# Layer-norm sums as rows, VectorE in place of GpSimd, and turns and moves in fours

## The chip, the cores and the metric

One Trainium2 chip, one of its cores. The kernel is one program with one launch; the metric is its device time in microseconds (us). The core has five engines with instruction streams of their own: TensorE (PE) for matrix products, VectorE (DVE), ScalarE (ACT), GpSimd (POOL) and SyncE (SP), which here issues the loads of weights. A profiled execution has a trace of all of them.

## What is computed

One decoder layer on 256 tokens with 16 meta tokens ahead of them (T = 272), width 2048, all in float32. Cut to what matters here:

```
h = concat(meta, x)
q, c_kv, q_idx, k_idx, w_idx, u = split_columns(h @ w_in)
c_kv = rms_norm(c_kv, kv_norm_g)                # per token, over 256 channels
...                                             # sparse attention, multi-scale pooling
mix = concat(attn_out, pool_out) @ w_o
h = layer_norm(ALPHA * h + mix, ln1_g, ln1_b)   # per token, over 2048 channels
z = causal depthwise conv of width 3 over tokens (h @ w_up) + conv_b
f = (gelu(z[:, :FF]) * z[:, FF:]) @ w_down      # FF = 5632
out = layer_norm(ALPHA * h + f, ln2_g, ln2_b)[16:]
```

`rms_norm` divides by the root of the mean square, `layer_norm` subtracts the mean and divides by the standard deviation; both need, for each token, sums over all channels.

## The kernel before

**Layout.** Activations lie transposed: channels on the 128 partitions, tokens along the free dimension. `y[:, m, :]` is the m-th of 16 tiles of 128 channels. From the output projection on, NQ = 258 token columns are kept (two of the meta tokens, for the convolution, and the 256). A sum over channels is therefore a sum over partitions.

**Products.** Each float32 operand is split into a rounded upper part and a remainder, and a product is three matmuls (upper by upper, upper by lower, lower by upper): `product`, L195 to L197, 16 channel tiles deep, so 48 matmuls per block. Weights stream from HBM in tiles of 1 MB in a fixed order (`stream`); SP loads a tile, ACT makes the upper halves (L123) and DVE the lower ones (L124), two pieces of each per tile. `weights()` hands out the next tile and starts the work on the one two ahead; there are three buffers for raw tiles and three for split ones. `behind(i)` is a context: what is issued inside it on ACT or DVE is put behind the split of tile i on that engine. For the rest the instructions' order on each engine is laid out when the program is built, by priority and modelled readiness, and is not exactly that of the code. Each engine then works through its order.

**The RMS norm of the latent.** `latent_scale` (after the first indexer block) squares two channel tiles and sums them over partitions with `column_sums`: the tile is the stationary operand, a block of 64 ones moves, so that the sums of up to 128 tokens come out with tokens on partitions; three cuts of tokens make a 128x3 tile. `pow(-0.5)` on POOL gives the scale. `latent_norm` (one block later) turns this into a row of all tokens on every partition with `spread`: products of the broadcast scale with the identity.

**The first layer norm** is folded into the first four pairs of up-projection blocks (FOLDED = 4; a pair is f, with half 0 and 1 of the gate). `about_k(m)` subtracts a rough mean, adds the tile to `s1` and its square to `s2` (two halves of one buffer `sums`, on POOL), and makes the operand `folded`, scaled by the norm's gain. PE can then start the first up blocks before mean and deviation are known. In the first of them, after 8 of the 16 channel tiles, `deviation()` sums `s1` and `s2` over partitions (`column_sums`, L242), and computes mean and 1/deviation with tokens on partitions; after 15 tiles `deviation_rows()` spreads both with L248 and ACT copies them (L696) to `rs` and `m2`, halves of `of_token`. Two things follow from them. `normalise(m)` makes the true h of tile m: POOL multiplies by `rs` (L704), DVE adds `m2` (L705), ACT applies gain and bias (L706) and splits (L708), DVE subtracts (L709); three tiles per block, behind the next split. `unfold(ps)` corrects a folded block: DVE multiplies by `rs` (L732), ACT makes `w` from `m2` (L734), POOL adds (L735). From f = 4 on, blocks use the true h.

**Turns and moves.** The residual for the second norm has tokens on partitions. DVE turns each 32x32 block of y (L886, after the gates of f = 4 and 5, eight tiles each), and 32 DMAs on ACT's queue (`residual`, L716) move the blocks to `y2`; six, five and five of them after the gates of f = 6 to 11. Then the down projection adds to `y2` with a fast scheme of seven products (`seven`, L787 to L789, L795).

Of the kernel before, what the change touches and what calls it, by code (L numbers as in the profile page):

```python
# [11 lines left out]
F32 = mybir.dt.float32  # L12
F32R = mybir.dt.float32r
AF = mybir.ActivationFunctionType
# [3 lines left out]
P = 128  # L18
# [24 lines left out]
REPLACED = -3e38  # L43
KA = NM + P
KB = T
KW = KA + KB
STRIP = 400
G_KV, G_POOL, LN1, C_W, C_B, N_COLS = 0, 2, 10, 42, 306, 394
# [19 lines left out]
def tile_layer(ctx, tc, xt, w_first, w_proj, w_uk, w_uv, w_pool, w_o, w_up, w_down, cols, rows, rel_bias, onehot, out):  # L68
# [163 lines left out]
    half = sb.tile([P, 3], F32, name="half")  # L232
    nc.vector.memset(half, -0.5)

    def col(base, j):
        return cv[:, base + j:base + j + 1]

    def column_sums(s, cuts, j, ps):

        for i, (a, b) in enumerate(cuts):  # L240
            for n, t in enumerate(s):
                nc.tensor.matmul(ps[:b - a, 64 * (3 * j + i):64 * (3 * j + i) + 64], t[:, a:b], ones[:, :64],  # L242
                                 start=n == 0, stop=n == len(s) - 1)

    def spread(r, cuts, rb):

        for i, (a, b) in enumerate(cuts):
            nc.tensor.matmul(rb[:, a:b], r[:b - a, i:i + 1].to_broadcast([b - a, P]), ident[:b - a, :b - a],  # L248
                             start=True, stop=True)

    def temp(shape, name):
        return ap_.tile(shape, F32, tag="t", name=name, bufs=4, padded_shape=[P, KW])
# [35 lines left out]
    for j in range(2):  # L288
        ps = heads[1 + j][0]
        nc.scalar.activation(ct[:, j, :], ps[:, :T], AF.Copy)  # L290
        sq = temp([P, T], "sq")
        nc.scalar.activation(sq, ps[:, :T], AF.Square)
        sqs.append(sq)
    widx = ap_.tile([P, 2, HI], F32, name="widx")
    ps = small()
# [5 lines left out]
    cuts = ((0, P), (P, 2 * P), (2 * P, T))  # L301
    v = sb.tile([P, 3], F32, name="rms_v")

    def latent_scale():
        ps = small()
        column_sums(sqs, cuts, 0, ps)
        nc.vector.memset(v, 1.0)
        for i, (a, b) in enumerate(cuts):
            nc.vector.tensor_scalar(v[:b - a, i:i + 1], ps[:b - a, 64 * i:64 * i + 1], 1.0 / C, EPS,
                                    op0=ALU.mult, op1=ALU.add)  # L310
# [322 lines left out]
    of_token = fp.tile([P, 2 * NQ], F32, name="of_token", tag="u2", bufs=1)  # L633
    rs, m2 = of_token[:, :NQ], of_token[:, NQ:]
    folded = []

    def about_k(m):
# [32 lines left out]
                about_k(len(folded))  # L670


    cuts = ((0, P), (P, 2 * P), (2 * P, NQ))
    st = fp.tile([P, 4, 3], F32, name="st", bufs=1)
    nc.vector.memset(st, 1.0)

    def deviation():
        ps = small()
        column_sums([s1], cuts, 0, ps)
        column_sums([s2], cuts, 1, ps)  # L680
        for i, (a, b) in enumerate(cuts):
            r = slice(0, b - a)
            nc.vector.tensor_scalar_mul(st[r, 0, i:i + 1], ps[r, 64 * i:64 * i + 1], 1.0 / D)
            nc.vector.tensor_scalar(st[r, 1, i:i + 1], ps[r, 64 * (3 + i):64 * (3 + i) + 1], 1.0 / D, EPS,
                                    op0=ALU.mult, op1=ALU.add)
        nc.vector.tensor_tensor(st[:, 2, :], st[:, 0, :], st[:, 0, :], op=ALU.mult)
        nc.vector.tensor_tensor(st[:, 1, :2], st[:, 1, :2], st[:, 2, :2], op=ALU.subtract)
        nc.vector.tensor_tensor(st[:2, 1, 2:], st[:2, 1, 2:], st[:2, 2, 2:], op=ALU.subtract)
        nc.gpsimd.tensor_tensor(st[:, 2, :], st[:, 1, :], half, op=ALU.pow)
        nc.vector.scalar_tensor_tensor(st[:, 3, :], st[:, 0, :], -1.0, st[:, 2, :], op0=ALU.mult, op1=ALU.mult)  # L690

    def deviation_rows():
        for j, dst in ((2, rs), (3, m2)):
            ps = small()
            spread(st[:, j, :], cuts, ps)
            nc.scalar.activation(dst, ps[:, :NQ], AF.Copy)  # L696


    y2 = fp.tile([P, 2, D], F32, name="y2", bufs=1)
# [1 line left out]

    def normalise(m):
        yd = y[:, m, Q0:]
        nc.gpsimd.tensor_tensor(yd, yd, rs, op=ALU.mult)  # L704
        nc.vector.tensor_tensor(yd, yd, m2, op=ALU.add)  # L705
# [3 lines left out]
        nc.vector.tensor_tensor(a[:, 1, :NQ], yd, a[:, 0, :NQ].bitcast(F32), op=ALU.subtract)  # L709
        h_parts.append(a)  # L710
# [16 lines left out]
    def unfold(ps):  # L727

        sc = fp.tile([P, 2], F32, name="sc", tag="sc")
        nc.vector.tensor_copy(sc, ps[:, NQ:NE])  # L730
        u = fp.tile([P, NQ], F32, name="u", tag="sq")
        nc.vector.tensor_tensor(u, ps[:, :NQ], rs, op=ALU.mult)  # L732
        w = fp.tile([P, NQ], F32, name="w", tag="acc", bufs=1, padded_shape=[P, 4 * P])
        nc.scalar.activation(w, m2, AF.Identity, bias=sc[:, 1:], scale=sc[:, :1])  # L734
        nc.gpsimd.tensor_tensor(u, u, w, op=ALU.add)  # L735
        return u

    def gate(za, zg):
# [37 lines left out]
    def seven(kind, part, c, j):  # L776
# [18 lines left out]
            nc.vector.scalar_tensor_tensor(to, to, 1.0 if part else ALPHA, ps, op0=ALU.mult, op1=ALU.add)  # L795

        if kind == "A":
            held["u"] = fp.tile([P, 512], F32, name="u", tag="u1", bufs=1, padded_shape=[P, 2 * NQ])
            nc.scalar.activation(held["u"], held["P1"], AF.Copy)
            held["v"] = fp.tile([P, 512], F32, name="v", tag="u2", bufs=1, padded_shape=[P, 2 * NQ])  # L800
            nc.scalar.activation(held["v"], held["P5"], AF.Copy)
            add(c11, held["P2"])
            add(c12, held["P3"])
            nc.gpsimd.dma_start(c11, held["u"], accum_op=ALU.add)
            nc.gpsimd.dma_start(c12, held["v"], accum_op=ALU.add)
        else:
            u, v = held["u"], held["v"]
            add(c22, v)
            nc.vector.tensor_tensor(u, u, held["P6"], op=ALU.add)
            nc.vector.tensor_tensor(v, u, held["P7"], op=ALU.add)  # L810
            add(c21, held["P4"])
            nc.gpsimd.dma_start(c12, u, accum_op=ALU.add)
            nc.gpsimd.dma_start(c21, v, accum_op=ALU.add)
            nc.gpsimd.dma_start(c22, v, accum_op=ALU.add)
# [4 lines left out]
    for item in plan:  # L819
# [37 lines left out]
        if f < FOLDED:  # L857
            k = 0
            if f + half_ == 0:
                product(ps[:, :NE], hl, P, folded, 0, NE, k1=8)  # L860
                deviation()
                product(ps[:, :NE], hl, P, folded, 0, NE, k0=8, k1=15)
                deviation_rows()
                k = 15
            product(ps[:, :NE], hl, P, folded, 0, NE, k0=k)
            with behind(state["use"]):
                while len(h_parts) < min(KT, 3 * (2 * f + half_ + 1)):
                    normalise(len(h_parts))
            both.append(ps)
            if half_ == 0:  # L870
                continue
            both = [conv(i * FT + f, i, unfold(both[i]), pair[:, f % 2]) for i in range(2)]
        else:
            product(ps[:, :NQ], hl, P, h_parts, 0, NQ)
            both.append(conv(half_ * FT + f, half_, ps, pair[:, f % 2]))
            if half_ == 0:
                continue
        gate(*both)
# [2 lines left out]
            gated.append(two_parts(a[:, :, :S], both[0]))  # L881
        elif f % 2:
            todo.append((part, pair))
        if f in (FOLDED, FOLDED + 1):
            for m in range(8 * (f - FOLDED), 8 * (f - FOLDED) + 8):
                nc.vector.transpose(y[:, m, NM:], y[:, m, NM:])  # L886
# [31 lines left out]
    def squares(i, q):  # L918

        a, b = piece(i, q)  # L920
        sq = fp.tile([P, 512], F32, name="sq", tag="u1" if q % 2 else "u2", bufs=1, padded_shape=[P, 2 * NQ])
# [159 lines left out]
```

## Time and profile before

| | |
|---|---|
| median of 3 runs | 1047.12 us (1046.78 to 1047.15) |
| profiled execution, its own time | 1047.53 us |
| its span, first to last instruction | 1045.7 us |
| TensorE clock granted | 0.998 of full |
| busy | PE 1036.5, DVE 886.3, ACT 623.1, POOL 217.9 us |
| HBM | 232.50 MB read, 2.11 MB written |

A row of a group reads: line, engine, operation, out<-in with shapes, xcount, then busy time of the group in us, mean of one in ns, the idle time of the engine just before them, and what ended it. A row of the order of time reads: start and length in us, engine, line, operation. "x12" behind a row says that twelve instructions were merged. A float32 product counts as two matmul instructions.

### The profile page before, as it was taken

Reading aid. Unit: us, or ns where it says so; the run is one execution under the profiler, and the core shown is the slowest. Engines: PE = TensorE matmul, PEld = TensorE weight load, DVE = VectorE, ACT = ScalarE, POOL = GpSimd, SP = SyncE. Lnnn points to the kernel's source line nnn. Section 1 sums busy time; section 2 is a strip of 40 time slices with the busy share of each in tenths; the row PEclk is TensorE's granted clock in tenths of the full one; section 3 lists DMA queues with packets and bytes.
Section 4 is the critical chain, followed back from the end, with each engine's and each line's share of the span. In section 5 each row is a group of like instructions: output and inputs, shape, how many; then the busy total and the mean of one; then the engine's idle time right before and its main releaser. Section 6 shows DMA issues by size and latency. Waiting matters only on the chain.

```text
span 1045.7 us, 19275 instructions
## 1 busy us (share of the span) xinstructions
PE 1036.5 (99%) x7673; PEld 986.5 (94%) x7673; DVE 886.3 (85%) x1380; ACT 623.1 (60%) x1002; POOL 217.9 (21%) x269
## 2 busy tenths in 40 slices
PE   9999999999999999999999999999999999999997
PEld 8999999999999999999999999999999999999986
DVE  6879568758769997899989989889898998989876
ACT  6656346645447765565565655656555666555665
POOL 1300014125345321111112011120111212220031
PEclk9999999999999999999999999999999999999999
DMA  8565643454552577998887787877878778787875
GB/s 320 207 224 211 219 154 112 150 184 167 186 198 85 198 226 229 274 301 281 279 285 273 267 285 268 291 269 277 276 269 282 277 285 276 263 286 270 294 211 162
DMA packets 59754, 250.28 MB, mean 239 GB/s; under 512 B 21734, under 2 KB 22416, under 8 KB 32656
## 3 DMA queue, kind: packets, MB, share of 16 engines
q1 hardware_dynamic: 34592, 230.42, 60.8%
q0 software_dynamic: 7888, 16.14, 8.1%
q10 hardware_dynamic: 17184, 2.49, 1.4%
q8 instruction: 60, 0.98, 0.4%
q14 instruction: 30, 0.25, 0.1%
HBM read 232.50 MB, written 2.11 MB: 224 GB/s over the span
## 4 chain that ended last, share of the span: by engine, by line
PE 61%; DVE 3%; issue 2%; DMA 1%; POOL 1%; ACT 1%; POOLq 0%; DVEq 0%; ACTq 0%
PE mm L196 15%; PE mm L197 15%; PE mm L195 15%; PE at L788 5%; PE at L787 5%; PE at L789 5%; DMA wraw<-in_w_down 1%; DVE whl L124 1%; POOL gb L901 0%; DVE hp L709 0%; DVE whl_r L143 0%; POOL u L735 0%; DVE x L705 0%; POOL y L960 0%; DVE za L723 0%
## 5 line engine op out<-in xcount | busy, mean ns | idle before, releaser
L124 DVE TENSOR_TENSOR whl<-wraw,whl 128x1024 fp32r<-128x1024 f32 (+1 forms) x416 | 487.8, 1207 | 38.1 <-ACT whl L123 37.1
L123 ACT ACTIVATE whl<-wraw 128x1024 fp32r<-128x1024 f32 (+1 forms) x416 | 402.1, 1015 | 104.0 <-DVE wraw L119 23.4
L196 PE MATMUL mm<-hp,whl 128*128 128x258 f32 x1280 | 362.4, 283 | 0.0
L195 PE MATMUL mm<-hp,whl 128*128 128x258 f32 x1280 | 361.5, 282 | 0.0
L197 PE MATMUL mm<-hp,whl 128*128 128x258 f32 x1280 | 361.3, 282 | 0.0
L196 PEld LDWEIGHTS mm<-hp,whl 128*128 128x128 f32 x1280 | 242.7, 190 | 3.1
L195 PEld LDWEIGHTS mm<-hp,whl 128*128 128x128 f32 x1280 | 242.5, 189 | 3.2
L197 PEld LDWEIGHTS mm<-hp,whl 128*128 128x128 f32 x1280 | 242.9, 190 | 0.0
L195 PE MATMUL mm<-xp,whl 128*128 128x256 f32 (+5 forms) x384 | 111.8, 291 | 0.0
L196 PE MATMUL mm<-xp,whl 128*128 128x256 f32 (+5 forms) x384 | 108.9, 284 | 0.0
L197 PE MATMUL mm<-xp,whl 128*128 128x256 f32 (+5 forms) x384 | 108.7, 283 | 0.0
L722 ACT ACTIVATE z<-mm,cv 128x256 f32<-128x256 f32 x40 | 22.6, 564 | 95.3 <-PE mm L197 95.0
L196 PEld LDWEIGHTS mm<-xp,whl 128*128 128x128 f32 x384 | 72.4, 188 | 0.8 <-issue 0.5
L195 PEld LDWEIGHTS mm<-xp,whl 128*128 128x128 f32 x384 | 72.4, 189 | 0.6
L197 PEld LDWEIGHTS mm<-xp,whl 128*128 128x128 f32 x384 | 72.4, 189 | 0.3 <-DVE whl L124 0.2
L788 PE MATMUL at<-whl,gp 128*128 128x512 f32 x180 | 71.2, 396 | 0.0
L789 PE MATMUL at<-whl,gp 128*128 128x512 f32 x180 | 71.1, 395 | 0.0
L787 PE MATMUL at<-whl,gp 128*128 128x512 f32 x180 | 71.1, 395 | 0.0
L762 POOL TENSOR_TENSOR forms<-za 128x128 f32<-128x128 f32 x20 | 24.8, 1238 | 215.5 <-DVE za L740 209.7
L722 ACT ACTIVATE za<-mm,cv 128x256 f32<-128x256 f32 x40 | 22.6, 564 | 73.5 <-PE mm L197 71.3
L759 POOL TENSOR_TENSOR forms<-za 128x128 f32<-128x128 f32 x20 | 21.7, 1087 | 110.1 <-DVE za L740 105.1
L789 PEld LDWEIGHTS at<-whl,gp 128*128 128x128 f32 x180 | 33.8, 188 | 8.0
(348 smaller groups left out, 1948.7 us busy)
## 6 DMA issues: line engine op xcount, KB each, us to landing
wraw<-in_w_up SPq DMA_DIRECT2D x88, 1024.0 KB, 5.0
wraw<-in_w_down SPq DMA_DIRECT2D x80, 1024.0 KB, 6.2
wraw<-in_w_proj SPq DMA_DIRECT2D x24, 1024.0 KB, 5.0
wraw<-in_w_o SPq DMA_DIRECT2D x16, 1024.0 KB, 4.9
y<-v POOLq DMA_DIRECT2D x27, 256.0 KB, 8.3
y<-u POOLq DMA_DIRECT2D x18, 256.0 KB, 4.9
wraw<-in_w_first SPq DMA_DIRECT2D x8, 304.0 KB, 5.5
x<-in_xt SPq DMA_DIRECT2D x1, 2176.0 KB, 9.0
```

What stands on the lines that cost most here:

```text
L123: upper = nc.scalar.activation(hl[:, 0, c], raw[:, c], AF.Copy)
L124: lower = nc.vector.tensor_tensor(hl[:, 1, c], raw[:, c], hl[:, 0, c].bitcast(F32), op=ALU.subtract)
L195: nc.tensor.matmul(ps, wh, ah, start=n == 0, stop=False)
L196: nc.tensor.matmul(ps, wh, al, start=False, stop=False)
L197: nc.tensor.matmul(ps, wl, ah, start=False, stop=n == KT - 1)
L722: nc.scalar.activation(z, src[:, 2:NQ], AF.Identity, bias=col(C_B, j), scale=col(C_W, 3 * j + 2))
L759: nc.gpsimd.tensor_tensor(s[:, 0], a21, a22, op=ALU.add)
L762: nc.gpsimd.tensor_tensor(s[:, 3], a11, a21, op=ALU.subtract)
L787: nc.tensor.matmul(ps, a[:, 0, i], hl[:, 0, w], start=j == 0, stop=False)
L788: nc.tensor.matmul(ps, a[:, 0, i], hl[:, 1, w], start=False, stop=False)
L789: nc.tensor.matmul(ps, a[:, 1, i], hl[:, 0, w], start=False, stop=j == n - 1)
```

## The change

- The sums over channels are made by one product per tile with the ones as the stationary operand and the squares as the moving one (`sum_rows`): every partition then holds the row of sums for all tokens. W = 288 is the token count rounded up to 32; the 16 or 30 columns behind the tokens are zeroed, or are the neighbouring buffer's.
- DVE turns such a row in 32x32 blocks (`to_partitions`), so that in every 32nd column a token's sum stands on partitions; mean and deviation are then computed on 128x9 tiles; DVE turns the result, broadcast, back into rows (`to_row`). The products with the identity (`spread`) and `deviation_rows` are gone.
- In `normalise` the multiplication, and in `unfold` the addition, are made by DVE instead of POOL. `normalise` runs two tiles per block instead of three.
- The 16 turns of y are issued four in each of the blocks of f = 4 and 5, and the 32 moves four in each of the eight blocks of f = 6 to 9, all behind the split of the next weight.

```diff
+W = (T + 31) // 32 * 32
...
+    def sum_rows(s):
+        ps = small()
+        for n, t in enumerate(s):
+            nc.tensor.matmul(ps[:, :W], ones, t, start=n == 0, stop=n == len(s) - 1)
+        return ps[:, :W]
+    def to_partitions(r, row):
+        nc.vector.transpose(r, row)
+    def to_row(r, v):
+        nc.vector.transpose(r.rearrange("p (a b) -> p a b", b=32), v[:, :, None].to_broadcast([P, W // 32, 32]))
...
     def latent_scale():
-        ps = small()
-        column_sums(sqs, cuts, 0, ps)
-        ...
+        r = temp([P, W], "r")
+        to_partitions(r, sum_rows(sqs))
+        nc.vector.tensor_scalar(v, r[:, ::32], 1.0 / C, EPS, op0=ALU.mult, op1=ALU.add)
         nc.gpsimd.tensor_tensor(v, v, half, op=ALU.pow)
     def latent_norm():
-        rb = small()
-        spread(v, cuts, rb)
+        rb = temp([P, W], "rb")
+        to_row(rb, v)
...
-    sums = fp.tile([P, 2 * NQ], F32, name="sums", tag="u1", bufs=1)
-    s1, s2 = sums[:, :NQ], sums[:, NQ:]
+    sums = fp.tile([P, NQ + W], F32, name="sums", tag="u1", bufs=1)
+    nc.gpsimd.memset(sums[:, 2 * NQ:], 0.0)
+    s1, s2 = sums[:, :NQ], sums[:, NQ:2 * NQ]
...
     def deviation():
-        ps = small()
-        column_sums([s1], cuts, 0, ps)
-        column_sums([s2], cuts, 1, ps)
-        ...
+        mean, square = (of_token[:, j * NQ:j * NQ + W] for j in range(2))
+        for j, r in enumerate((mean, square)):
+            to_partitions(r, sum_rows([sums[:, j * NQ:j * NQ + W]]))
+        ...
+        for j in range(2):
+            to_row(of_token[:, j * NQ:j * NQ + W], st[:, 2 + j, :])
-    def deviation_rows():
-        ...
...
     def normalise(m):
-        nc.gpsimd.tensor_tensor(yd, yd, rs, op=ALU.mult)
+        nc.vector.tensor_tensor(yd, yd, rs, op=ALU.mult)
...
     def unfold(ps):
-        nc.gpsimd.tensor_tensor(u, u, w, op=ALU.add)
+        nc.vector.tensor_tensor(u, u, w, op=ALU.add)
...
                 deviation()
-                product(ps[:, :NE], hl, P, folded, 0, NE, k0=8, k1=15)
-                deviation_rows()
-                k = 15
+                k = 8
             product(ps[:, :NE], hl, P, folded, 0, NE, k0=k)
             with behind(state["use"]):
-                while len(h_parts) < min(KT, 3 * (2 * f + half_ + 1)):
+                while len(h_parts) < min(KT, 2 * (2 * f + half_ + 1)):
                     normalise(len(h_parts))
...
             both.append(conv(half_ * FT + f, half_, ps, pair[:, f % 2]))
+            with behind(state["use"]):
+                b = 2 * (f - FOLDED) + half_
+                for m in range(4 * b, 4 * b + 4):
+                    if m < KT:
+                        nc.vector.transpose(y[:, m, NM:], y[:, m, NM:])
+                for _ in range(4):
+                    if moves and b > 3:
+                        residual(*moves.pop(0))
...
-        if f in (FOLDED, FOLDED + 1):
-            for m in range(8 * (f - FOLDED), 8 * (f - FOLDED) + 8):
-                nc.vector.transpose(y[:, m, NM:], y[:, m, NM:])
-        if FOLDED + 2 <= f < FOLDED + 8:
-            for _ in range((6, 5, 5)[f % 3]):
-                residual(*moves.pop(0))
```

More of the change, by code (lines that the diff above doesn't have):

```diff
@@ L231, in tile_layer @@
     nc.vector.memset(ones, 1.0)
-    half = sb.tile([P, 3], F32, name="half")
+    half = sb.tile([P, W // 32], F32, name="half")
     nc.vector.memset(half, -0.5)
@@ L236, in col @@
         return cv[:, base + j:base + j + 1]
[L238 to L249, printed above, removed]
+    def sum_rows(s):
[7 more added lines that the diff above has]
+        nc.vector.transpose(r.rearrange("p (a b) -> p a b", b=32), v[:, :, None].to_broadcast([P, W // 32, 32]))
     def temp(shape, name):
@@ L290, in tile_layer @@
         nc.scalar.activation(ct[:, j, :], ps[:, :T], AF.Copy)
-        sq = temp([P, T], "sq")
-        nc.scalar.activation(sq, ps[:, :T], AF.Square)
+        sq = temp([P, W], "sq")
+        nc.gpsimd.memset(sq[:, T:], 0.0)
+        nc.scalar.activation(sq[:, :T], ps[:, :T], AF.Square)
         sqs.append(sq)
@@ L300, in tile_layer @@
     ctp = ap_.tile([P, 2, 2, T], F32R, name="ctp", tag="q")
-    cuts = ((0, P), (P, 2 * P), (2 * P, T))
-    v = sb.tile([P, 3], F32, name="rms_v")
+    v = sb.tile([P, W // 32], F32, name="rms_v")
     def latent_scale():
-        ps = small()
-        column_sums(sqs, cuts, 0, ps)
[L307 to L310, printed above, removed]
+        r = temp([P, W], "r")
+        to_partitions(r, sum_rows(sqs))
+        nc.vector.tensor_scalar(v, r[:, ::32], 1.0 / C, EPS, op0=ALU.mult, op1=ALU.add)
         nc.gpsimd.tensor_tensor(v, v, half, op=ALU.pow)
     def latent_norm():
-        rb = small()
-        spread(v, cuts, rb)
+        rb = temp([P, W], "rb")
+        to_row(rb, v)
         for j in range(2):
@@ L630, in tile_layer @@
     acc = fp.tile([P, NQ], F32, name="acc", tag="acc", bufs=1, padded_shape=[P, 4 * P])
-    sums = fp.tile([P, 2 * NQ], F32, name="sums", tag="u1", bufs=1)
-    s1, s2 = sums[:, :NQ], sums[:, NQ:]
-    of_token = fp.tile([P, 2 * NQ], F32, name="of_token", tag="u2", bufs=1)
-    rs, m2 = of_token[:, :NQ], of_token[:, NQ:]
+    sums = fp.tile([P, NQ + W], F32, name="sums", tag="u1", bufs=1)
+    nc.gpsimd.memset(sums[:, 2 * NQ:], 0.0)
+    s1, s2 = sums[:, :NQ], sums[:, NQ:2 * NQ]
+    of_token = fp.tile([P, NQ + W], F32, name="of_token", tag="u2", bufs=1)
+    rs, m2 = of_token[:, :NQ], of_token[:, NQ:2 * NQ]
     folded = []
@@ L670, in tile_layer @@
                 about_k(len(folded))
-    cuts = ((0, P), (P, 2 * P), (2 * P, NQ))
-    st = fp.tile([P, 4, 3], F32, name="st", bufs=1)
-    nc.vector.memset(st, 1.0)
+    st = fp.tile([P, 4, W // 32], F32, name="st", bufs=1)
     def deviation():
-        ps = small()
-        column_sums([s1], cuts, 0, ps)
-        column_sums([s2], cuts, 1, ps)
[L681 to L685, printed above, removed]
+        mean, square = (of_token[:, j * NQ:j * NQ + W] for j in range(2))
+        for j, r in enumerate((mean, square)):
+            to_partitions(r, sum_rows([sums[:, j * NQ:j * NQ + W]]))
+        mean, square = mean[:, ::32], square[:, ::32]
+        nc.vector.tensor_scalar_mul(st[:, 0, :], mean, 1.0 / D)
         nc.vector.tensor_tensor(st[:, 2, :], st[:, 0, :], st[:, 0, :], op=ALU.mult)
-        nc.vector.tensor_tensor(st[:, 1, :2], st[:, 1, :2], st[:, 2, :2], op=ALU.subtract)
-        nc.vector.tensor_tensor(st[:2, 1, 2:], st[:2, 1, 2:], st[:2, 2, 2:], op=ALU.subtract)
+        nc.vector.scalar_tensor_tensor(st[:, 1, :], square, 1.0 / D, st[:, 2, :], op0=ALU.mult, op1=ALU.subtract)
+        nc.vector.tensor_scalar(st[:, 1, :], st[:, 1, :], 0.0, EPS, op0=ALU.max, op1=ALU.add)
         nc.gpsimd.tensor_tensor(st[:, 2, :], st[:, 1, :], half, op=ALU.pow)
         nc.vector.scalar_tensor_tensor(st[:, 3, :], st[:, 0, :], -1.0, st[:, 2, :], op0=ALU.mult, op1=ALU.mult)
-    def deviation_rows():
[L693 to L696, printed above, removed]
+        for j in range(2):
+            to_row(of_token[:, j * NQ:j * NQ + W], st[:, 2 + j, :])
     y2 = fp.tile([P, 2, D], F32, name="y2", bufs=1)
@@ L920, in squares @@
         a, b = piece(i, q)
-        sq = fp.tile([P, 512], F32, name="sq", tag="u1" if q % 2 else "u2", bufs=1, padded_shape=[P, 2 * NQ])
+        sq = fp.tile([P, 512], F32, name="sq", tag="u1" if q % 2 else "u2", bufs=1, padded_shape=[P, NQ + W])
         nc.scalar.activation(sq[:, :b - a], y2[:, i, a:b], AF.Square, bias=mvs[i][:, 2:3],
```

4 lines of the change are left out of this document (2 added, 2 removed).

## The prediction

> **What bounds the kernel now.** I read the page first, then the list of who waited for whom on TensorE, then the order of time around the four places that the change touches on PE, then VectorE (DVE) in the stage where it is fullest.
>
> ```profile
> span 1045.7 us, 19275 instructions
> PE 1036.5 (99%) x7673; PEld 986.5 (94%) x7673; DVE 886.3 (85%) x1380; ACT 623.1 (60%) x1002; POOL 217.9 (21%) x269
> ```
>
> TensorE (PE) is busy for 1036.5 of 1045.7 us. A busy PE need not be a PE at its peak, so the second question is whether it waits inside the stages:
>
> ```profile
> PE at L972 <- ACT diag L970: 1.5, 1, 1.5
> ...
> PE mm L197 <- DVE whl L124: 0.6, 2, 0.4
> ```
>
> Of the waits that the profile can name, the longest lies at the end (L972), which the change does not touch. The only other one that matters here is 0.6 us in which two products waited for DVE's half of a weight split (L124). So time is won by taking work out of PE's stream, and lost where another engine makes PE wait.
>
> **PE's own terms.** The price of a product is read from the starts of its neighbours, because the matmuls are pipelined. The model for the new sums is the one float32 product of 128x258 with the ones that exists already:
>
> ```profile
> 240.54 0.60 PE L666 MATMUL at<-acc,ones 128*128 128x258 f32 x2
> 240.79 0.47 PE L195 MATMUL mm<-mixp,whl 128*128 128x258 f32 x1
> 241.10 0.29 PE L196 MATMUL mm<-mixp,whl 128*128 128x258 f32 x1
> 241.22 0.29 PE L197 MATMUL mm<-mixp,whl 128*128 128x258 f32 x1
> ```
>
> Neighbouring products of the stream start 0.12 us apart (241.10 to 241.22). From 240.54 to 241.10 are 0.56 us; one product of the stream (L195) lies in it, so the sum took 0.56 - 0.12 = 0.44 us of PE. The new sums stream W = 288 columns: I estimate 0.44 x 288 / 258 = 0.49 us each. The same subtraction prices what goes. First the RMS norm of the latent, its sums and its spreading:
>
> ```profile
> 30.00 1.32 PE L242 MATMUL at<-ones,sq 128*128 128x64 f32 x12
> 31.26 0.39 PE L195 MATMUL mm<-xp,whl 128*128 128x256 f32 x1
> 31.48 0.28 PE L196 MATMUL mm<-xp,whl 128*128 128x256 f32 x1
> ...
> 38.01 0.93 PE L248 MATMUL at<-ident,rms_v 128*128 128x128 f32 x6
> 38.87 0.39 PE L195 MATMUL mm<-xp,whl 128*128 128x256 f32 x1
> 39.09 0.28 PE L196 MATMUL mm<-xp,whl 128*128 128x256 f32 x1
> ```
>
> The column sums cost 31.48 - 30.00 - 0.12 = 1.36 us and become two products of 0.49, so 0.38 is saved. The spreading costs 39.09 - 38.01 - 0.12 = 0.96 and goes to DVE, so 0.96 is saved. Then the first layer norm, with the GpSimd (POOL) row that makes its last input:
>
> ```profile
> 306.28 1.62 POOL L648 TENSOR_TENSOR sums<-sums,sq 128x258 f32<-128x258 f32 x1
> ...
> 307.33 1.55 PE L242 MATMUL at<-ones,sums 128*128 128x64 f32 x12
> 308.82 0.39 PE L195 MATMUL mm<-fold,whl 128*128 128x260 f32 x1
> 309.04 0.28 PE L196 MATMUL mm<-fold,whl 128*128 128x260 f32 x1
> ...
> 311.43 1.86 PE L248 MATMUL at<-ident,st 128*128 128x128 f32 x12
> 313.22 0.39 PE L195 MATMUL mm<-fold,whl 128*128 128x260 f32 x1
> 313.44 0.29 PE L196 MATMUL mm<-fold,whl 128*128 128x260 f32 x1
> ```
>
> The sums cost 309.04 - 307.33 - 0.12 = 1.59 us. Two new ones are 0.98. But a wait comes in: each new product takes 288 columns from a buffer whose halves are 258 wide, so the sum over s1 also reads the first 30 columns of s2, and s2 is finished only at 306.28 + 1.62 = 307.90. Today six products over s1 stand in front and hide that. Now PE waits from 307.33 to 307.90, 0.57 us, unless the order of issue puts the sums later; behind it wait the remaining products of this block. I take the wait: 1.59 - 0.98 - 0.57 = 0.04 saved, and 0.61 without it. The spreading costs 313.44 - 311.43 - 0.12 = 1.89 us and leaves PE wholly.
>
> PE's sum is 0.38 + 0.96 + 0.04 + 1.89 = 3.27 us saved, or 3.84 without the wait.
>
> **VectorE's account, where the cover may fail.** All PE terms of the layer norm lie in front of the stage in which DVE is full. These are DVE's groups of instructions between 313.8 and 355.1 us (the rest of the four folded blocks), the page's row of all splits, and the windows:
>
> ```profile
> L124 DVE TENSOR_TENSOR whl<-wraw,whl 128x1024 fp32r<-128x1024 f32 x12 | 15.0, 1266 | 0.0
> L709 DVE TENSOR_TENSOR hp<-x,hp 128x258 fp32r<-128x258 f32 x16 | 9.5, 624 | 0.0
> L705 DVE TENSOR_TENSOR x<-x,of_token 128x258 f32<-128x258 f32 x16 | 8.9, 587 | 0.0
> L732 DVE TENSOR_TENSOR u<-mm,of_token 128x258 f32<-128x258 f32 x6 | 2.5, 411 | 0.0
> L723 DVE SCALAR_TENSOR_TENSOR za<-u,cv,za 128x256 f32<-128x256 f32 x3 | 2.4, 800 | 0.0
> L886 DVE STREAM_TRANSPOSE x<-x 128x256 f32<-128x256 f32 x5 | 2.2, 432 | 0.0
> ...
> L723 DVE SCALAR_TENSOR_TENSOR z<-u,cv,z 128x256 f32<-128x256 f32 x3 | 1.4, 474 | 0.0
> ...
> L730 DVE COPY sc<-mm 128x2 f32<-128x2 f32 x6 | 0.9, 148 | 2.6 <-PE mm L197 2.6
> ```
>
> ```profile
> L124 DVE TENSOR_TENSOR whl<-wraw,whl 128x1024 fp32r<-128x1024 f32 (+1 forms) x416 | 487.8, 1207 | 38.1 <-ACT whl L123 37.1
> ...
> L704 POOL TENSOR_TENSOR x<-x,of_token 128x258 f32<-128x258 f32 x16 | 13.9, 905 | 1.8 <-ACT of_token L696 1.8
> ...
> L735 POOL TENSOR_TENSOR u<-u,w 128x258 f32<-128x258 f32 x8 | 10.1, 1261 | 28.5 <-ACT w L734 16.5 <-DVE u L732 9.4 <-issue 2.6
> ```
>
> ```profile
> 313.80:355.10 41.30, 40.68 (x337) 40.26 (x336) 41.21 (x74) 33.91 (x61) 20.17 (x21) 1.00 0.36 128
> ...
> 376.00:400.00 24.00, 24.00 (x203) 24.00 (x201) 21.36 (x33) 13.85 (x24) 4.10 (x5) 1.00 0.79 245
> 400.00:434.00 34.00, 34.00 (x246) 32.17 (x245) 26.07 (x35) 18.84 (x26) 3.64 (x4) 1.00 0.78 238
> ```
>
> The windows' columns are length, then busy time of PE, weight load, DVE, ACT and POOL. In the first, DVE is busy 41.21 of 41.30 us: nothing is free, and both of PE's waits for a split belong here. Into this stage the change puts 16 multiplications (L704) and, as L732 runs six times in it, 6 additions (L735). What they cost on DVE I read from L732, the same shape on the same engine: 0.41 us, so 22 x 0.41 = 9.0 us more. What goes: beside POOL's work L705 took 587 and L709 624 ns, where 411 is the price of L732; with POOL silent I expect 16 x 0.41 = 6.6 for each, so 8.9 - 6.6 = 2.3 and 9.5 - 6.6 = 2.9 back. L723 on za falls to the row of z, 2.4 - 1.4 = 1.0. The splits fall to the mean of all, 12 x 1.207 = 14.5, so 0.5 back. The five turns (L886), 2.2 us, leave the stage, because the change queues them behind splits of later blocks. The balance is 9.0 - 2.3 - 2.9 - 1.0 - 0.5 - 2.2 = +0.1 us: even. Spacing the normalisation at two instead of three per block takes pressure from the first blocks, and the last two parts come in the last folded block.
>
> The new turns that replace the spreading (four of 288 columns, by L886's 0.43 us for 256 about 0.49 each, 2.0 together) fall into the 2.6 us in which DVE waits for PE ahead of L730, where six small operations also go. If that cover is gone, they cost DVE 2.0, not PE at once. The RMS norm's four turns stand at 30 to 40 us, where nobody needs the latent for 40 us; the power on POOL works on 9 instead of 3 columns: between 0 and a few tenths, on a chain that PE does not wait for. The memsets are early on an idle POOL: nothing.
>
> ```profile
> ACT za L722 <- POOL u L735: 4.2, 2, 3.5
> ```
>
> This row, ACT's waits from 304 to 356 us, speaks for a gain: ACT stood for 3.5 us because POOL, sixteen multiplications deep, came late to its first addition (L735), and ACT's halves of the splits (L123) were queued behind that wait. With the addition on DVE this goes. So the 0.6 us of PE's waits could vanish or, with DVE still full, stay. I take half, 0.3. Sum: 3.27 + 0.3 = 3.6 us.
>
> **Turns and moves.**
>
> ```profile
> L716 ACTq DMA_DIRECT2D y<-x x32: 592/593/2030, 367.4 to 465.0; - x32
> ```
>
> The moves are 32 DMAs issued from ACT's queue, 0.59 us each, today six, five and five per pair of blocks until 465 us. Now four per block, from about 376 us, finished after eight blocks. Four blocks lie in 376 to 400: 16 x 0.59 = 9.5 us of issuing beside 13.85 of ACT work is 23.3 of 24.0. It fits, and each stands behind the split of the next weight, so I put it at 0; if it did not fit, up to 9.5 us of later ACT work, splits among it, would slip in a stretch where PE waits for none today (24.00 of 24.00). The sixteen turns then lie behind 355 us, where eleven of them run already; the five that are added there are the 2.2 us counted above, at the start of a stretch in which DVE has time free again (21.36 of 24.00 from 376 us). From 355 us to the end PE sets the pace, so a gain made before it is kept.
>
> **Forecast and its base.** The profiled execution took 1047.53 us beside its span of 1045.7; the median of the runs is 1047.12, 0.41 lower. 1047.53 - 3.6 = 1043.9 for such an execution, 1043.5 by the median; I say 1043.6. About 0.2% (2.1 us) is what the measurement can tell from no change.
>
> **Rivals.** *DVE sets the pace of the folded blocks* (chance 0.16). Its account is even but full, so what PE no longer does there (1.89 + 0.04 + 0.3) turns into waits for L124, and only the latent's 0.38 + 0.96 = 1.34 is kept: 1047.12 - 1.3 = 1045.8, within 0.2%. For it: 41.21 of 41.30. Against: the turns leave, and the start of the stage has 2.6 us of idle.
>
> *DVE is parked in the unfolding* (0.11, slower). The added L735 needs ACT's w (L734). POOL waited 16.5 us for it in all, at no cost since POOL had nothing else. If the addition stands on DVE straight behind the multiplication, the splits stand behind the same wait. The bounds are 0 (other work is issued between) and 16.5. It decides from 3.6 us on, where the gain is eaten; at half of the bound, 8.2, PE waits for splits and the time is 1047.1 - 3.3 + 8.2 = 1052.
>
> *No relief* (0.05, slower). If L705, L709, L723 and L124 stay as long as they are now, the balance is 9.0 - 2.2 = 6.8 us more on a full DVE, and the time 1047.1 - 3.3 + 6.8 = 1050.6. Against it stands that L705 took 587 ns where L732 took 411. [...]
>
> *The change does not do what it says* (0.02): the issue order is not the order of the code, for five turns (L886), written after the fifth gate, run among the folded blocks already; if they stayed there, 2.2 us stay in the stage and the first rival's time results.
>
> **Chances and range.** My forecast has 0.66. Faster by over 0.2% is the forecast, 0.66; within it the first rival and the last, 0.18; slower the two on DVE, 0.16. The lower end takes PE's 3.84, all 0.6 and some 0.4 for the spread of runs: 1047.1 - 4.8 = 1042.3. The upper end takes in the first rival and a little parking, 1047.2, and leaves the slower cases out. The forecast's own range is 1042.3 to 1044.9.
>
> **What would show it.** Two products of two passes each in place of the 24 and no L248; PE's wait for s2 near 307 us, about 0.6; L705 and L709 near 411 ns; POOL without the two additions; turns after 355 us and moves ended by some 435. Wrong: PE waiting for L124 by more than 1 us between 314 and 355, or DVE idle behind ACT's w.

## The result and the profile after

The change made the kernel slower. Its median is 1055.14 us (1052.64 to 1057.78 in six runs) against 1047.05 us for the kernel before in the same session: a ratio of 1.0079, 95% interval 1.0060 to 1.0097. The profiled execution took 1056.32 us with a span of 1054.4. The forecast was 1043.6, so about 11.5 us separate the two.

The head of the page, and after it the list of who waited on TensorE (engine and product, what it waited for, us in total, times, longest), both of the changed kernel:

```profile
span 1054.4 us, 19205 instructions
...
PE 1037.2 (98%) x7639; PEld 985.2 (93%) x7639; DVE 886.7 (84%) x1401; ACT 623.1 (59%) x1000; POOL 196.2 (19%) x248
```

```profile
PE at L781 <- DVE whl L125: 7.0, 4, 3.3
...
PE mm L197 <- DVE hp L702: 0.7, 1, 0.7
...
PE at L243 <- POOL sums L650: 0.5, 1, 0.5
```

No engine has much more to do than before: PE 1037.2 against 1036.5 us, DVE 886.7 against 886.3. The three waits shown are new; two smaller new ones, of 0.5 and 0.3 us, are left out. The largest, 7.0 us, is of the down projection's products (L781) for lower halves of their weights (L125). The windows show where it lies. The columns are length, then busy time of PE, weight load, DVE, ACT and POOL, the granted clock, the DMA share and GB/s; first the kernel before, then the changed one:

```profile
410.00:460.00 50.00, 50.00 (x360) 47.22 (x360) 44.44 (x62) 30.04 (x41) 5.34 (x7) 1.00 0.90 277
```

```profile
410.00:460.00 50.00, 42.59 (x272) 37.97 (x271) 33.75 (x45) 24.50 (x34) 9.06 (x6) 0.93 0.68 204
```

The loss sits between 410 and 460 us. There PE is idle for 7.4 us and its clock is 0.93; DVE, which it waits for, works 33.75 us in place of 44.44. An engine that others wait for and that is itself less busy must be waiting. DVE in order of time, before and then after (start, length, line, operation, in brackets the idle time ahead and what ended it):

```profile
415.82 0.68 DVE L115 TENSOR_TENSOR wraw<-wraw 128x512 f32<-128x512 f32 x1
...
417.68 1.23 DVE L124 TENSOR_TENSOR whl<-wraw,whl 128x1024 fp32r<-128x1024 f32 x1 [0.26 <-ACT whl L123]
...
419.16 1.22 DVE L124 TENSOR_TENSOR whl<-wraw,whl 128x1024 fp32r<-128x1024 f32 x1
423.29 0.69 DVE L115 TENSOR_TENSOR wraw<-wraw 128x512 f32<-128x512 f32 x1 [2.91 <-DMA wraw<-in_w_down]
```

```profile
411.77 0.69 DVE L116 TENSOR_TENSOR wraw<-wraw 128x512 f32<-128x512 f32 x1 [2.00 <-DMA wraw<-in_w_down]
412.38 4.62 DVE L125 TENSOR_TENSOR whl<-wraw,whl 128x1024 fp32r<-128x1024 f32 x4
...
418.02 0.42 DVE L733 TENSOR_TENSOR za<-za,z 128x256 f32<-128x256 f32 x1
423.38 0.69 DVE L116 TENSOR_TENSOR wraw<-wraw 128x512 f32<-128x512 f32 x1 [4.94 <-DMA wraw<-in_w_down]
423.99 4.62 DVE L125 TENSOR_TENSOR whl<-wraw,whl 128x1024 fp32r<-128x1024 f32 x4
```

Some tiles of the down projection need a combination of their parts on DVE (L116 or L119 to L121, before L115) ahead of their split. Before, the tile that is combined at 415.82 has its lower halves at 417.68 and 419.16, and only then does DVE stand for the next down tile's load. In the changed kernel a tile is combined at 411.77, and ACT has its upper halves ready at 417.5:

```profile
415.54 1.99 ACT L124 ACTIVATE whl<-wraw 128x1024 fp32r<-128x1024 f32 x2
```

Its lower halves come at 423.99, 6.5 us later. In front of them in DVE's queue stands the combination of the next down tile, whose load lands at 423.4; DVE stands for 4.94 us beside work that is ready. The chain of waits runs through just this place:

```profile
412.38 4.63 DVE whl L125 x4
417.03 6.33 DMA wraw<-in_w_down
423.42 0.57 issue
423.99 1.23 DVE whl L125
425.27 0.80 PE at L781
```

It sustains itself: the late lower halves also free the raw buffer late, so the next load is issued late (between 400 and 460 us the queue of the loads waits up to 10.8 us for lower halves, before the change up to 7.4), and the combination that stands first waits longer (2.00 us at 411.77, 4.94 at 423.38, then 7.30 at 436.83).

The instruction order on DVE, as each program was built, can be counted. For each of the first eight such down tiles: how many earlier tiles (up tiles among them) still have lower halves behind its first combination.

```
before             1 1 0 1 0 1 0 0
changed kernel     2 2 2 2 2 1 0 0
```

The second cost is the clock. Windows of the changed kernel around its two long stalls:

```profile
422.20:424.70 2.50, 0.40 (x2) 0.00 (x0) 1.32 (x2) 1.14 (x3) 0.00 (x0) 1.00 0.45 96
424.70:428.10 3.40, 2.83 (x8) 2.35 (x9) 3.40 (x4) 1.96 (x2) 0.00 (x0) 0.50 0.35 57
...
435.00:438.40 3.40, 0.44 (x2) 0.00 (x0) 1.57 (x2) 0.52 (x2) 0.00 (x0) 0.99 0.48 89
438.40:441.80 3.40, 3.08 (x8) 2.59 (x9) 3.40 (x4) 0.00 (x0) 0.00 (x0) 0.50 0.33 77
```

Each is followed by 3.4 us at half the clock (0.50). The products of the down projection start 0.42 us apart in it (426.29 to 426.71) and 0.23 us behind it (428.30 to 428.53). PE is busy for 2.83 and 3.08 us of them; I estimate from the clock that this is work of 1.4 and 1.5 us at the full one, so the half clock costs 3.0 us in all. The account of the profiled execution: the first product with the true h starts 4.2 us earlier than before and the end is 8.8 us later (1056.32 - 1047.53), so 13.0 us are lost between. Of these 0.7 are the new wait for hp (L702) at 356 us, 7.4 the stalls between 410 and 460, and 3.0 the half clock; 1.9 are not assigned.

### The profile page after: what moved, and what is told of

It is laid out like the page before. It is cut to its first block, busy times and chain, and to the rows that moved or that the text cites. A ratio compares the mean times of both kernels' runs of the same rounds, so it can differ in the third digit from the quotient of the medians.

```text
span 1054.4 us, 19205 instructions
## 1 busy us (share of the span) xinstructions
PE 1037.2 (98%) x7639; PEld 985.2 (93%) x7639; DVE 886.7 (84%) x1401; ACT 623.1 (59%) x1000; POOL 196.2 (19%) x248
## 4 chain that ended last, share of the span: by engine, by line
PE 82%; DVE 9%; DMA 3%; issue 3%; ACT 2%; POOL 1%; ACTq 0%; SPq 0%; POOLq 0%; DVEq 0%
PE mm L197 19%; PE mm L196 19%; PE mm L198 19%; PE at L781 5%; PE at L782 5%; PE at L780 5%; DVE whl L125 4%; DMA wraw<-in_w_down 2%; PE mm L831 1%; PE mm L832 1%; PE mm L830 1%; ACT whl L124 1%; PE mm L267 1%; DVE hp L702 1%; DMA y<-x 0%
## 5 line engine op out<-in xcount | busy, mean ns | idle before, releaser
L125 DVE TENSOR_TENSOR whl<-wraw,whl 128x1024 fp32r<-128x1024 f32 (+1 forms) x416 | 486.7, 1206 | 38.6 <-ACT whl L124 37.6
L781 PE MATMUL at<-whl,gp 128*128 128x512 f32 x180 | 73.0, 407 | 6.2 <-DVE whl L125 6.2
L715 ACT ACTIVATE z<-mm,cv 128x256 f32<-128x256 f32 x40 | 22.5, 563 | 89.0 <-PE mm L198 88.9
L752 POOL TENSOR_TENSOR forms<-za 128x128 f32<-128x128 f32 x20 | 25.6, 1278 | 209.6 <-DVE za L733 143.8
L755 POOL TENSOR_TENSOR forms<-za 128x128 f32<-128x128 f32 x20 | 23.8, 1190 | 206.2 <-DVE za L733 192.9
L715 ACT ACTIVATE za<-mm,cv 128x256 f32<-128x256 f32 x40 | 22.5, 562 | 66.1 <-PE mm L198 62.7
L781 PEld LDWEIGHTS at<-whl,gp 128*128 128x128 f32 x180 | 34.8, 193 | 14.0 <-DVE whl L125 7.5
```

Source lines behind the costliest of these rows:

```text
L125: lower = nc.vector.tensor_tensor(hl[:, 1, c], raw[:, c], hl[:, 0, c].bitcast(F32), op=ALU.subtract)
L715: nc.scalar.activation(z, src[:, 2:NQ], AF.Identity, bias=col(C_B, j), scale=col(C_W, 3 * j + 2))
L752: nc.gpsimd.tensor_tensor(s[:, 0], a21, a22, op=ALU.add)
L755: nc.gpsimd.tensor_tensor(s[:, 3], a11, a21, op=ALU.subtract)
L781: nc.tensor.matmul(ps, a[:, 0, i], hl[:, 1, w], start=False, stop=False)
```

## The experiments

The theory: the moves' and turns' new places change the order that the builder lays out on DVE, and this order alone costs the time. The rivals: the moves themselves cost it, by holding ACT (four issues in a row, 2.65 us; "issue" in the expectations) or by delaying the loads with their small packets ("traffic"); the turns do; or the norm's work on DVE does ("VectorE"). All ratios are against the kernel before, run in the same session on the same chip.

**Moves in the old place.**

```diff
-                for _ in range(4):
-                    if moves and b > 3:
-                        residual(*moves.pop(0))
...
+        if FOLDED + 2 <= f < FOLDED + 8:
+            for _ in range((6, 5, 5)[f % 3]):
+                residual(*moves.pop(0))
```

> The changed kernel with the 32 moves back in their old place (six, five and five after the gates of f = 6 to 11); the turns stay in fours. Theory 'order': with the moves in fours, the program's order on VectorE has the first combination of the down tile i+2 ahead of the lower halves of tile i (five down tiles in a row), VectorE stands for a load while a finished tile waits, and PE runs out of weights near 420, 435 and 455 us. Here three down tiles, not in a row, still have it so: 1044 to 1047 us, PE waits of 0 to 3 us there. Rival 'issue' (ScalarE held by four DMA issues in a row): 1043.6. Rival 'VectorE' (the multiplications, additions and turns that it took over): 1055 still.

Measured: 1055.77 us, 1.0094 [1.0073, 1.0114], above the 1044 to 1047 that the theory gave. TensorE's waits:

```profile
PE at L780 <- DVE y L788: 3.6, 1, 3.6
PE at L781 <- DVE whl L125: 2.7, 2, 2.5
```

Two things stood in for the one removed. Three down tiles still had two tiles behind their first combination (1 1 0 2 0 2 0 2), and a wait appeared that neither kernel had, for the last moved slab of y (L788). Where the moves stand does not explain the time alone; two causes had to be parted.

**Turns in the old place.**

```diff
-                for m in range(4 * b, 4 * b + 4):
-                    if m < KT:
-                        nc.vector.transpose(y[:, m, NM:], y[:, m, NM:])
...
+        if f in (FOLDED, FOLDED + 1):
+            for m in range(8 * (f - FOLDED), 8 * (f - FOLDED) + 8):
+                nc.vector.transpose(y[:, m, NM:], y[:, m, NM:])
```

> The changed kernel with the sixteen turns back after the gates of f = 4 and 5; the moves stay in fours. 'Order', 'issue' and 'traffic' (the moves' small packets delay the loads): 1055 as the changed kernel, stalls at the same places. 'Turns' (they alone upset VectorE): under 1047.

Measured: 1055.22 us, 1.0079 [1.0064, 1.0094], the order on DVE as in the changed kernel (2 2 2 2 2 1), and the wait for L125 8.2 us. The turns are not the cause.

**The order held, all else as changed.** The first combination of a down tile is put behind the lower halves of the tile two before it:

```diff
-        split[i] = fetch(raw, hl, stream[i], kinds.get(i))
+        with ExitStack() as queued:
+            if kinds.get(i) and i - 2 in split:
+                queued.enter_context(tc.issue_after(getattr(split[i - 2][1], "ins", split[i - 2][1])))
+            split[i] = fetch(raw, hl, stream[i], kinds.get(i))
```

> The changed kernel, moves in fours, with one edge more: the combinations of down tile i stand behind the lower halves of tile i-2 on VectorE. Nothing else is edited; ScalarE issues the same moves at the same points. 'Order': the waits near 420 to 456 us go, 1043.5 to 1045.5 us, no clock drop. 'Issue' and 'traffic': the moves still hold ScalarE and the DMA engines, 1050 to 1055.

Measured: 1045.04 us (1043.47 to 1049.89, ten runs), 0.9983 [0.9972, 0.9995]. The order is 1 1 0 0 0 1, and the same stretch of DVE, ACT's issues in it and the window read:

```profile
413.96 0.68 DVE L116 TENSOR_TENSOR wraw<-wraw 128x512 f32<-128x512 f32 x1
...
415.96 2.42 DVE L125 TENSOR_TENSOR whl<-wraw,whl 128x1024 fp32r<-128x1024 f32 x2 [0.40 <-ACT whl L124]
418.64 2.36 DVE L125 TENSOR_TENSOR whl<-wraw,whl 128x1024 fp32r<-128x1024 f32 x2 [0.25 <-ACT whl L124]
...
421.82 0.69 DVE L116 TENSOR_TENSOR wraw<-wraw 128x512 f32<-128x512 f32 x1 [0.42 <-DMA wraw<-in_w_down]
```

```profile
411.82 2.70 ACTq L712 DMA_DIRECT2D y<-x  x4
```

```profile
410.00:460.00 50.00, 50.00 (x358) 47.10 (x358) 44.52 (x62) 29.14 (x41) 5.78 (x7) 1.00 0.94 281
```

No instruction was taken away and the four issues in a row on ACT are still there; only the order differs, and 10 us come back. That the moves hold ACT, or delay the loads by their packets, is ruled out as the cause.

**Turns and moves alone, added to the kernel before**, with the order left to the builder and then with the same edge:

> The kernel before with the turns and moves of the change alone (sums, normalisation and unfolding as before). 'Order' and 'issue': the loss alone, without the 3.4 us that the start of the up stage won, 1047 + 8 to 11 = 1055 to 1058 us. 'VectorE': about 1047.

> The kernel before with the turns and moves in fours, and the edge that puts the combinations of down tile i behind the lower halves of tile i-2. 'Order': the loss of moves_only (10.6 us) goes, 1046 to 1048.5. 'Issue' and 'traffic': 1055 and more stay.

Measured: 1057.79 us, 1.0102 [1.0085, 1.0118], order 1 2 2 2 2 1; with the edge 1047.37 us, 1.0003 [0.9994, 1.0013]. So turns and moves cost 10.6 us (1057.79 - 1047.16) by the order, and no loss by their work can be measured. This also parts the change in two: with the order held, the norm's half is worth 1047.37 - 1045.04 = 2.3 us, or 2.1 by the ratios.

**The order alone, provoked in the kernel before.** Loads and combinations are written ahead of the split, and the lower halves of tile i - 2 are put behind the first combination of tile i, for the first five down tiles:

```diff
...
+        with ExitStack() as queued:
+            if i + 2 in early:
+                queued.enter_context(tc.issue_after(getattr(firsts[i + 2], "ins", firsts[i + 2])))
+            split[i] = halves(raw, hl, kinds.get(i))
```

> The kernel before; its moves, turns, sums and normalisation untouched. Only the order on VectorE is provoked: for the first five down tiles the lower halves of tile i-2 are put behind the first combination of tile i (four of the five then stand two tiles ahead, as five do in the changed kernel). 'Order': PE waits for lower halves between 400 and 460 us, 1051 to 1057 us. If the moves or the new VectorE work were needed for the loss: 1047.

Measured: 1054.18 us, 1.0070 [1.0052, 1.0088], with the order 2 2 2 1 2 0. TensorE's waits and the windows around the longest:

```profile
PE at L806 <- DVE whl L129: 2.9, 2, 2.6
```

```profile
415.20:418.60 3.40, 0.77 (x4) 0.43 (x4) 3.40 (x5) 2.73 (x4) 0.00 (x0) 1.00 0.23 39
418.60:422.00 3.40, 3.40 (x9) 2.62 (x8) 2.08 (x4) 0.00 (x0) 0.46 (x1) 0.51 0.76 253
```

Turns, moves and norms are those of before here, and 6.7 us are lost (1054.18 - 1047.44), in the same stretch, by the same wait and the same halved clock (0.51). The order alone suffices. What stood in front need not be a load: DVE waited 4.62 us for a load ahead of the combination at 401.91, but just before the longest stall it waited 1.84 us for an upper half of ACT ahead of an up tile at 414.14, while a down tile's lower halves stood behind.

**The moves on GpSimd's queue**, all else as changed:

```diff
-        nc.scalar.dma_start(to, y[src, :, t:t + 32])
+        nc.gpsimd.dma_start(to, y[src, :, t:t + 32])
```

> The changed kernel with the 32 moves issued from GpSimd's queue instead of ScalarE's, at the same places. Built so, the order on VectorE has no combination two tiles ahead. 'Order': 1043.5 to 1045.5. 'Traffic' (the same packets at about the same times): 1052 to 1056.

Measured: 1044.54 us (1043.36 to 1046.44, nine runs), 0.9976 [0.9966, 0.9986]. No edge is in it; the builder, with ACT's queue free of the moves, laid out 1 1 0 0 0 0 by itself. That shows that the moves on ACT bring the bad order about in this kernel. By which of its estimates the builder does so was not tried.

**A stricter edge**: every down tile's first combination behind the lower halves of the tile directly before it (i - 1 in the diff above).

> The changed kernel with a stricter edge: the combinations of down tile i stand behind the lower halves of tile i-1. 'Order': PE waits for no split after 356 us, and less scatter than with i-2 (1043.5 to 1049.9 there), since a late load then holds back nothing that is ready: 1043.3 to 1044.5. If the strict order makes the combinations themselves late, over 1046.

Measured: 1046.43 us, 0.9993 [0.9982, 1.0003], against the 1043.3 to 1044.5 that was expected; it lies where the combinations themselves were to be late ("over 1046"). With all counts at 0 the profiled execution has two waits of 0.2 us for L125 after 356 us, at 440.5 and 447.3 us. The intervals of this edge and the one before overlap, so the runs do not tell the two apart; they do not show either that one tile ahead, as in the kernel before, costs anything. Two ahead does.

**Moves in the old place with the order held** undoes both things that were left over in the first experiment:

> The changed kernel with its moves in the old place (behind the unfolding's blocks, five or six at a time) and with the order of the splits held: the first combination of a down tile stands behind the lower halves of the tile two before it. It undoes two things at once, and so tells whether the two that moves_back left over are independent. Theory (the order of issue on VectorE costs the time; where the moves stand costs it only through that order, and by being late for the unfolding): no stall for lower halves between 411 and 456 us; the unfolding's wait for a late moved slab, 3.6 us at 475 in moves_back, stays if lateness is due to the place (about 1044 + 3.6 + up to 1.7 for a halved clock = 1047 to 1049.5), and goes if it was the late splits that made it (1044). Rival (the place of the moves itself is what costs, through ScalarE): between 1042.5 and 1044, below order_fixed's 1045.04.

Measured: 1050.71 us, 1.0042 [1.0028, 1.0055], a little above the range of 1047 to 1049.5. All waits for L125 are gone, and one is left in this stretch:

```profile
PE at L783 <- DVE y L791: 3.5, 1, 3.5
```

```profile
DMA to landing us min/median/max: 2.2/6.8/10.1
```

The second row is from the view of the tile y between 380 and 500 us. The last three moves are issued at 462.2 to 463.5 and land up to 10.1 us later, at 473.6; PE reaches the product that needs them at 471.6. In the kernel before the last one landed at 471.9 and PE's block came 2.8 us later (its start is at 472.6, here at 469.8). So moving them earlier is needed once PE is ahead; left in the old place, they cost 3.5 us of stall and a lower clock behind it (0.58 from 475.10 to 478.50). That settles the miss of the first experiment: two independent causes.

**Towards a better kernel.** With the moves on GpSimd's queue, `deviation` after ten channel tiles in place of eight (for PE's wait for s2), and the normalisation two parts earlier:

```diff
-                product(ps[:, :NE], hl, P, folded, 0, NE, k1=8)
+                product(ps[:, :NE], hl, P, folded, 0, NE, k1=10)
...
-                while len(h_parts) < min(KT, 2 * (2 * f + half_ + 1)):
+                while len(h_parts) < min(KT, 2 * (2 * f + half_ + 2)):
```

> The changed kernel with the moves issued from GpSimd's queue (as in moves_pool, 1044.54), and with two waits of TensorE taken out ahead of it: the deviation's products stand behind ten folded tiles of the first accumulation in place of eight (0.5 to 0.6 us at about 306 us, for the sums of squares), and the normalisation is two parts earlier in VectorE's queue (0.7 to 0.84 us at about 356 us). Theory (what is left over before's chain are these two waits): 1044.54 - 0.6 - 0.8 = 1043.1, between 1042.3 and 1044. Rival (the normalisation two parts earlier pushes the splits behind it on VectorE, which is full between 311 and 353 us): a wait for lower halves of 0.5 to 1.5 us there, and 1044 to 1046.

> As pool_best, with the order of the splits held as well (the first combination of a down tile behind the lower halves of the tile two before it). Theory (the order is already as before's once the moves are off ScalarE's queue, so the edge has nothing left to do): as pool_best within 0.5 us. Rival (an order left over in the up tiles or in the first down tiles still costs): up to 1 us below pool_best.

> As pool_best, with the moves issued from SyncE's queue, behind the weight loads that stand there. Theory (any queue that is not ScalarE's, with the splits' order of before, does): as pool_best, 1042.3 to 1044. Rival (a move that waits for its turned slab holds the load behind it): loads land up to some us later than in pool_best between 400 and 440 us, a wait of TensorE for splits of 1 to 3 us there, and 1045 to 1049.

Measured: 1044.12 us (1043.37 to 1045.5, nine runs), 0.9973 [0.9964, 0.9983], just above the 1042.3 to 1044 expected; with the edge as well 1044.77 us, 0.9979 [0.9970, 0.9988]. Both beat the kernel before and the changed one, but neither is told apart from the plain move to GpSimd's queue. The wait for s2 is gone; the one for the last normalised tile grew from 0.7 to 1.1 us:

```profile
PE mm L197 <- DVE hp L702: 1.1, 1, 1.1
```

What was taken out at 306 us came back at 356; DVE is full between (41.66 of 42.00 us from 311 to 353).

On SyncE's queue the time is 1066.77 us, 1.0188 [1.0174, 1.0202], far off both expectations. The count on DVE is 0 for all tiles; this time ACT is the one that stands. Its order of time:

```profile
414.17 0.56 ACT L715 ACTIVATE z<-mm,cv 128x256 f32<-128x256 f32 x1 [6.20 <-PE mm L198]
414.63 1.05 ACT L124 ACTIVATE whl<-wraw 128x1024 fp32r<-128x1024 f32 x1
```

The tile whose upper halves begin at 414.63 had landed at 402.4. It stands behind an evacuation (L715) that waits 6.20 us for PE to end its block, and PE then waits for the tile. It is the same kind of loss on another engine: ready work behind a wait. This is read from the trace; no run holds ACT's order.

## Why the prediction was wrong

**PE's terms held.** The new sums, in order of time in the changed kernel, first of the RMS norm and then of the layer norm:

```profile
30.07 1.13 PE L243 MATMUL at<-sq,ones 128*128 128x288 f32 x4
...
31.16 0.28 PE L197 MATMUL mm<-xp,whl 128*128 128x256 f32 x1
```

```profile
305.94 0.28 PE L198 MATMUL mm<-fold,whl 128*128 128x260 f32 x1
306.68 1.24 PE L243 MATMUL at<-sums,ones 128*128 128x288 f32 x4 [0.47 <-POOL sums L650]
...
307.88 0.28 PE L197 MATMUL mm<-fold,whl 128*128 128x260 f32 x1
```

By the prediction's own subtraction the first cost 31.16 - 30.07 - 0.12 = 0.97 us (0.98 forecast). The second start 306.68 - 306.06 = 0.62 us late, the forecast wait for s2 of 0.57, and cost 307.88 - 306.68 - 0.12 = 1.08. No L248 is left.

**DVE's account held.** The folded stage in groups and its window, changed kernel:

```profile
L698 DVE TENSOR_TENSOR x<-x,of_token 128x258 f32<-128x258 f32 x15 | 6.2, 422 | 0.0
L702 DVE TENSOR_TENSOR hp<-x,hp 128x258 fp32r<-128x258 f32 x14 | 5.7, 422 | 0.0
L697 DVE TENSOR_TENSOR x<-x,of_token 128x258 f32<-128x258 f32 x14 | 5.7, 422 | 0.0
...
L728 DVE TENSOR_TENSOR u<-u,w 128x258 f32<-128x258 f32 x6 | 2.5, 425 | 0.0
```

```profile
313.80:355.10 41.30, 41.30 (x346) 41.30 (x346) 41.27 (x94) 35.24 (x60) 0.00 (x0) 1.00 0.47 158
```

The addition of m2 fell from 587 to 422 ns and the last subtraction from 624 to 422, where 411 was forecast. DVE is full and PE waits for nothing: 41.30 of 41.30, where before it was 40.68. The rivals of a DVE that sets the pace, of a DVE parked behind ACT's w (L728 has no idle time ahead), and of no relief are all refuted. These starts mark the gain, before and then after:

```profile
304.45 0.28 PE L195 MATMUL mm<-fold,whl 128*128 128x260 f32 x1
...
355.13 0.28 PE L195 MATMUL mm<-hp,whl 128*128 128x258 f32 x1
```

```profile
303.17 0.28 PE L196 MATMUL mm<-fold,whl 128*128 128x260 f32 x1
...
350.93 0.28 PE L196 MATMUL mm<-hp,whl 128*128 128x258 f32 x1
```

The first folded product is 1.28 us earlier (1.34 forecast), the first one with the true h 4.20 us (3.6 forecast; both waits for splits went, where half was taken, which is 0.3 of the 0.6 more).

**Small misses.** The power on POOL for the RMS norm took 2.73 us on nine columns against 1.78 on three (L311), 0.94 more where at most a few tenths were allowed; only DVE waited for it, 0.5 us (L252). The last normalised tiles were put "in the last folded block", and no cost was given for being last. PE waits 0.7 us for one (L702) at 356 us. 4.2 - 0.7 leaves 3.5 at that point. That the median with the order held is only 2.1 us below before's (1047.16 - 1045.04) is not settled: its profiled execution, 1043.47 us, lies where the forecast said, but it is the lowest of ten. The other runs reach 1049.89 (that one with a mean clock of 0.995, the others with 0.997 or 0.998), and what stalls in them no profile shows.

**The step that failed is "Turns and moves", "so I put it at 0".** The working asked whether ACT has the time for the issues, found 23.3 of 24.0 us, and named slipping splits on ACT as the only cost. What the runs showed in place of 0 is a loss of 10.6 us for turns and moves alone, by the order on DVE. With it fell "From 355 us to the end PE sets the pace": PE stood 7.4 us between 410 and 460. For the work itself 0 was right: turns and moves alone with the order held are 1.0003 [0.9994, 1.0013] of before. What was left out is that the order on every engine is laid out anew when the program is built. The text knew it ("the issue order is not the order of the code") but used it only to ask where five turns would land, at 0.02. No rival asked what a new order does to the neighbours of what is moved. The trace of before held the hint: DVE already stood 2.91 us for a load at 423.29 with one tile ahead. One tile more ahead, and the wait would have stood in front of lower halves that PE needs next. For the price that wait of 2.91 us gave a first size; in the changed kernel the waits grew to 4.94 and 7.30 us, which the trace of before could not tell.

## What to carry to other kernels

When a program's instruction order is laid out by a builder, an edit that costs nothing can still change the order that an engine works through: DVE kept to the order it was given here, and stood 4.94 us beside work that was ready. Compare the built order before and after on each engine, and look first at instructions that wait for a load. Where a queue mixes "ready now" with "when the load lands", hold the order with an edge (worth 10.1 us here, 1055.14 - 1045.04); a tighter edge than the good kernel's own order gained nothing that could be measured here. An engine that was waited for and was less busy than before pointed here at its order, not at its work.

## What was not expected of the hardware

The longest stalls of PE cost more than their length in these runs. After stalls of 2.7 and 3.3 us in the changed kernel the granted clock was 0.50 for 3.4 us each time. After one of 3.5 us it was 0.58 and then 0.92 in two neighbouring windows; if these are a mix of the full and the half clock, an estimate from them is some 3.4 us at half the clock (2 x 0.42 x 3.4 + 2 x 0.08 x 3.5):

```profile
475.10:478.50 3.40, 3.39 (x11) 2.79 (x12) 3.40 (x5) 0.00 (x0) 1.77 (x2) 0.58 0.37 64
478.50:482.00 3.50, 3.50 (x29) 3.50 (x29) 3.50 (x8) 1.84 (x2) 0.00 (x0) 0.92 0.96 222
```

(moves in the old place with the order held). Not every stretch with idle time was followed by this: in the changed kernel PE was busy for 0.50 of the 1.72 us from 455.80 to 457.52, and the clock was 1.00 up to 461.00; with the moves on SyncE's queue it was busy for 1.69 of the 3.40 us from 427.80 on, and the clock of the next 3.40 us was 1.00. The halved stretch did not start where the stall ended: in the changed kernel it starts at 424.70, while the stall ends at 425.27. Nor was PE always idle just ahead of it: in the kernel before with the provoked order, PE was busy for 0.77 of the 3.40 us ahead of the window with a clock of 0.51. What sets the half clock off, these runs do not show.
